# Order of the residual combinations, of one gate pair's operand loads and of a meta token's sums in a one-core encoder kernel

## The chip, the cores and the metric

The kernel runs on one core of a Trainium2 chip. The metric is device microseconds of one execution, lower is better. Before the change three executions took 2128.84, 2129.21 and 2135.24 us (median 2129.21).

## The reference

One encoder layer is applied to two sequences with shared weights: a long one of 1024 tokens and a short one of 512, each with 16 learned meta tokens in front, all in float32. Only what the change touches is quoted; the attention that makes `mix` lies ahead of it.

```python
D_MODEL, D_FF, N_META = 1024, 2816, 16

h = h + mix @ w_out                      # residual add behind the attention
n = rms_norm(h, g_ffn)
gate = n @ w_ff_gate                     # 1024 x 2816
pad = pad_by_one_position(gate)          # zero outside the sequence
gate = pad[:, :-2] * conv_w[0] + pad[:, 1:-1] * conv_w[1] + pad[:, 2:] * conv_w[2] + conv_b
h = h + (gelu(gate) * (n @ w_ff_up)) @ w_ff_down
y = rms_norm(h, g_final)[:, N_META:]     # the meta tokens are dropped at the end
```

Behind the attention only the last meta token still matters: the convolution at the first real token reads its gate.

## The kernel before, in words

Tensors are held transposed, with model columns on the 128 partitions and tokens along the free dimension. Every product is made of three fp32r matmuls: each operand is split into a high part (`split`, L114: a cast on ACT) and a low part (L115: a subtraction on DVE or POOL), and `mm3` (L121 to L123) multiplies high by high, low by high and high by low. The code is written as generators; a scheduler then sets the order of each engine's instructions, and each engine runs its own list strictly in that order. `behind(g, ins)` adds an ordering without a wait: what is issued in its block stands behind `ins` in the list of that instruction's engine.

For the long sequence `mixer_out_long` computes `h + mix @ w_out` in three thirds of each half of the tokens (`PARTS`: 170, 172 and 170 columns of each half, so tiles of 342, 344 and 340 columns). For each of eight row blocks `j` it loads the residual, runs 24 matmuls into a PSUM buffer `s` (there are three), adds the residual on DVE (L728), stores the block for later (L729) and adds up its squares. When a third is done, its generator `combine` takes the mean of squares on PE (L657), the inverse root (L103 to L107), scales the third (L667), and forms the seven operands of one Strassen-Winograd step: `x11, x21, x22` as they are and `t1` to `t4` as differences (L680), each split. `combine` is called `late` and is advanced two steps at a time between the row blocks of the next third, from `j = ML = 2` on. The combination of the last third runs beside the first gate products.

`conv_glu_long` then goes through the 22 blocks of the hidden width in 11 pairs. Each pair needs seven block products for the gate (`winograd`, 12 matmuls each, added up on DVE by L934 and L991) and seven for the up matrix. Gate operands of the first pair have been split and summed earlier and lie in DRAM as `g.wg`; `product` loads each as a high and a low tile of 256 KB (L923), through `HB` = 5 pairs of buffers. The first pair's gate runs in two chunks of columns: 342 columns (of the first two thirds) and 170 columns (of the last third). Each chunk loads all seven operands, 28 loads in all.

The gate of the last meta token is a matrix-vector product made outside of PE's main work: ACT scales the raw gate weights by the token's normalised vector (L977, eight instructions for each block of 128), DVE adds them up over the eight row blocks (L979), and a matmul with a constant column adds over the partitions (L1004). The raw gate weights of the first pair are loaded behind the 18th of the 28 loads (`g.loads[17:18]`).

Of the kernel before, what the change touches and what calls it, by code (L numbers as in the profile page):

```python
# [1 line left out]

# [1 line left out]

# [16 lines left out]
P = 128  # L21
# [618 lines left out]
def mixer_out_long(ctx, g, wp, x, begin):  # L640

    nc = g.nc
    hp = pool(ctx, g, "fh0", 2, "right")
    cm = max(2 * w + 2 * (o == 0) for o, w in PARTS)

    def halves(a, o, w):
        return a.rearrange("... (x t) -> ... x t", x=2)[..., o:o + w]

    def combine(o, w, cw, h, sums):
        ps = g.psum.tile(P, cw, "s")
        for i, sq in enumerate(sums):
            nc.tensor.matmul(ps, lhsT=g.ones_d, rhs=sq, start=i == 0, stop=i == len(sums) - 1)  # L657
        rstd = hp.tile([P, cm], F32, name="rstd", tag="rstd", bufs=1)[:, :cw]
        rsqrt_newton(g, hp, rstd, ps, cw)
        yield  # L660
        if not x:
            xp = begin()
            g.x0 = xp.tile([P, KT], F32, name="x0")
            x.update({nm: [xp.tile([P, HT, H], F32R, name=f"{nm}_{part}") for part in ("hi", "lo")] for nm in XS})
        for k in range(KT):
            hs = h[:, k, :2 * w]
            nc.vector.scalar_tensor_tensor(out=hs, in0=hs, scalar=g.gain[:, V_GFFN + k:V_GFFN + k + 1],  # L667
                                           in1=rstd[:, :2 * w], op0=ALU.mult, op1=ALU.mult)
            if k % 2:
                yield  # L670
        if cw > 2 * w:
            nc.vector.scalar_tensor_tensor(out=g.x0, in0=h[:, :, 2 * w], scalar=rstd[:, 2 * w:2 * w + 1],
                                           in1=g.gain[:, V_GFFN:V_GFFN + KT], op0=ALU.mult, op1=ALU.mult)
        (x11, x12), (x21, x22) = [[h[:, k:k + HT, i * w:(i + 1) * w] for i in range(2)] for k in (0, HT)]

        def kept(nm, src):
            split(g, x[nm][0][:, :, o:o + w], x[nm][1][:, :, o:o + w], src)

        def minus(out, a, b):
            nc.vector.tensor_tensor(out=out, in0=a, in1=b, op=ALU.subtract)  # L680

        kept("x11", x11)
        yield
        kept("x21", x21)
        yield
        minus(x11, x12, x11)
        kept("t1", x11)
        yield
        minus(x11, x22, x11)
        kept("t2", x11)  # L690
        yield
        minus(x12, x22, x12)
        kept("t3", x12)
        yield
        kept("x22", x22)
        minus(x21, x21, x11)
        kept("t4", x21)

    late = None
    with ExitStack() as es:  # L700
        mp = pool(es, g, "fm0", 2, "right")
        for o, w in PARTS:
            cw = 2 * w + 2 * (o == 0)
            xhi, xlo = [[mp.tile([P, cm], F32R, name=nm, tag=f"{nm}{k}", bufs=1 + (k >= KT - 2))[:, :cw] for k in range(KT)]
                        for nm in ("xhi", "xlo")]
            h = hp.tile([P, KT, cm], F32, name="h", tag="h")[:, :, :cw]
            acc = mp.tile([P, cm], F32, name="acc", tag="acc")[:, :cw]
            sums = [acc]

            def loaded(tag, bufs, real, meta):  # L710
                t = mp.tile([P, cm], F32, name=tag, tag=tag, bufs=bufs)[:, :cw]
                nc.sync.dma_start(out=t[:, :2 * w].rearrange("p (x t) -> p x t", x=2), in_=halves(real, o, w))
                if o == 0:

                    nc.sync.dma_start(out=t[:, 2 * w:2 * w + 1], in_=meta)
                    nc.vector.memset(t[:, 2 * w + 1:], 0.0)
                return t

            for k in range(KT - 1, -1, -1):
                rows = g.oT[0][k * P:(k + 1) * P]  # L720
                split(g, xhi[k], xlo[k], loaded("m", MB, rows[:, 1:], rows[:, 0:1]))
            for j in range(KT):
                wj = load_parts(g, wp, g.wo[j]) if j in PRE else load_halves(g, wp, g.w_out[j])
                rows = g.xT[0][j * P:(j + 1) * P]
                res = loaded("res", 2, rows[:, NMETA:], rows[:, NMETA - 1:NMETA])
                ps = g.psum.tile(P, cw, "s")
                dense(g, ps, wj, xhi, xlo, 0, cw, range(KT - 1, -1, -1))
                nc.vector.tensor_tensor(out=h[:, j], in0=ps, in1=res, op=ALU.add)  # L728
                nc.gpsimd.dma_start(out=halves(g.h[j], o, w),  # L729
                                    in_=h[:, j, :2 * w].rearrange("p (x t) -> p x t", x=2))  # L730
                if o == PARTS[-1][0] and j >= KT - 2:

                    sums.append(mp.tile([P, cm], F32, name="sq_p", tag="m", bufs=MB)[:, :cw])
                    nc.scalar.activation(sums[-1], h[:, j], AF.Square)
                else:
                    add_square(g, mp, acc, h, j, 0, cw, nc.gpsimd, 1)
                yield 24 * cw
                if late and j >= ML:
                    for _ in range(2):
                        next(late, None)  # L740
            if late:
                drain(late)
            late = combine(o, w, cw, h, sums)
        next(late)
    return late
# [149 lines left out]
    yield 0  # L895


def winograd(g, wp, up, x, raw, c0, cw, pre=None):

# [14 lines left out]
    def product(a, b, place):  # L916
        if pre is None:
            a = split_half(g, wp, a)
        else:
            i, half = place  # L920
            a = [wp.tile([P, H], F32R, name=nm, tag=nm, bufs=HB) for nm in ("w_hi", "w_lo")]
            for part, tl in enumerate(a):
                g.loads.append(nc.sync.dma_start(out=tl.bitcast(F32),  # L923
                                                 in_=pre[i, part, :, half * H:(half + 1) * H]).ins)
# [31 lines left out]
def conv_glu_long(ctx, g, wp, x, late, es_x, es_h):  # L956
# [6 lines left out]
    up = pool(es, g, "fu0", 2, "left")  # L963
    ap = None
    first = PARTS[-1][0]
    g.loads = []

    def load_gate(f0):


        with behind(g, *g.loads[17:18] if f0 == 0 else g.loads[-1:] if f0 == 2 else []):
            raw = [load_whole(wp, g, g.w_gate[f0 + i]) for i in range(2)]
        sums = []
        for i in range(2):
# [8 lines left out]
    for f0 in range(0, NFF, 2):  # L983
# [2 lines left out]
            raw, first_sums = load_gate(f0)  # L986

        for c0, cw in ((0, first), (first, H - first)) if f0 == 0 else ((0, H),):
            for i, half, ps, rest in winograd(g, wp, up, x, raw if f0 else None, c0, cw, None if f0 else g.wg):
                t0 = 1 + half * H + c0  # L990
                nc.vector.tensor_tensor(out=gate[:, i, t0:t0 + cw], in0=ps, in1=rest, op=ALU.add)  # L991
                for _ in range(3):
# [5 lines left out]
        if not ap:  # L998
            es_h.close()
            ap = pool(es, g, "fa0", 1, "left")  # L1000
        act = ap.tile([P, 2, N], F32, name="act", tag="act", bufs=2)
        for i in range(2):
            ps = g.psum.tile(P, 2, "mm")
            nc.tensor.matmul(ps, lhsT=first_sums[i], rhs=g.ones_d[:, 0:2], start=True, stop=True)  # L1004
# [12 lines left out]
        if f0 + 2 == NFF:  # L1017
            with tc.issue_after(gelu.ins):
                nc.scalar.preload_act_table_set(EXP_LN)
        raw = [load_whole(up, g, g.w_up[f0 + i], "w_f2") for i in range(2)]  # L1020
        for i, half, ps, rest in winograd(g, wp, up, x, raw, 0, H):
            a = act[:, i, half * H:(half + 1) * H]
            nc.vector.tensor_tensor(out=ps, in0=ps, in1=rest, op=ALU.add)
            nc.vector.tensor_tensor(out=a, in0=ps, in1=a, op=ALU.mult)
# [417 lines left out]
```

## Time and profile before

| | us |
|---|---|
| median of three executions | 2129.21 |
| their range | 2128.84 to 2135.24 |
| the profiled execution | 2138.1 |
| its span, first to last instruction | 2136.3 |
| PE busy in the span | 2051.1 (96%) |
| DVE busy | 1724.1 (81%) |
| ACT busy | 1156.8 (54%) |
| POOL busy | 582.7 (27%) |

The profiled execution is 8.9 us longer than the median of the others. PE, TensorE's matmuls, has work nearly all the time, so a microsecond is worth something where PE waits or where its clock is low. The granted clock is given as a share of full speed: 1.00 is 2.4 GHz and 0.50 is 1.2 GHz.

### The profile page before, as it was taken

Reading aid. Unit: us, or ns where it says so; the run is one execution under the profiler, and the core shown is the slowest. Engines: PE = TensorE matmul, PEld = TensorE weight load, DVE = VectorE, ACT = ScalarE, POOL = GpSimd, SP = SyncE. Lnnn points to the kernel's source line nnn. Section 1 sums busy time; section 2 is a strip of 40 time slices with the busy share of each in tenths; the row PEclk is TensorE's granted clock in tenths of the full one; section 3 lists DMA queues with packets and bytes.
Section 4 is the critical chain, followed back from the end, with each engine's and each line's share of the span. In section 5 each row is a group of like instructions: output and inputs, shape, how many; then the busy total and the mean of one; then the engine's idle time right before and its main releaser. Section 6 shows DMA issues by size and latency. Waiting matters only on the chain.

```text
span 2136.3 us, 35264 instructions
## 1 busy us (share of the span) xinstructions
PE 2051.1 (96%) x12302; PEld 1833.1 (86%) x12302; DVE 1724.1 (81%) x3786; ACT 1156.8 (54%) x2253; POOL 582.7 (27%) x534
## 2 busy tenths in 40 slices
PE   6999999999999999999999999979999999999998
PEld 6988888997887999899989999978888777778877
DVE  6878889767879788888988885578878878869886
ACT  6635566544657556666666765345444444435454
POOL 4653233553112000000000000542444444330112
PEclk8999999999999999999999999998999999999999
DMA  7564335456621322223352224986232232247443
GB/s 252 178 198 133 118 110 170 153 182 226 206 84 55 105 75 70 70 85 114 103 188 77 93 88 145 300 256 229 101 109 89 97 115 84 94 166 258 119 126 126
DMA packets 164897, 296.30 MB, mean 139 GB/s; under 512 B 21456, under 2 KB 82672, under 8 KB 164208
## 3 DMA queue, kind: packets, MB, share of 16 engines
q1 hardware_dynamic: 162416, 287.76, 41.6%
q0 software_dynamic: 2304, 6.29, 0.8%
q8 instruction: 97, 1.59, 0.3%
q14 instruction: 80, 0.66, 0.1%
HBM read 211.13 MB, written 82.85 MB: 138 GB/s over the span
## 4 chain that ended last, share of the span: by engine, by line
PE 76%; DVE 12%; DMA 4%; ACT 3%; issue 3%; POOL 1%; SPq 1%; DVEq 0%; ACTq 0%; POOLq 0%
PE ps_mm L121 17%; PE ps_mm L123 17%; PE ps_mm L122 17%; PE ps_t L456 5%; PE ps_s L431 3%; PE ps_s L432 3%; PE ps_s L121 2%; PE ps_s L122 2%; PE ps_s L123 2%; PE ps_o L471 2%; PE ps_o L470 2%; DVE p L433 1%; DVE w_lo L115 1%; DMA m<-oT 1%; DVE acc L979 1%
## 5 line engine op out<-in xcount | busy, mean ns | idle before, releaser
L121 PE MATMUL ps_mm<-xhi,w_hi 128*128 128x258 f32 (+3 forms) x1264 | 383.4, 304 | 12.0 <-ACT xhi L114 3.7
L122 PE MATMUL ps_mm<-xlo,w_hi 128*128 128x258 f32 (+3 forms) x1264 | 379.0, 300 | 0.3 <-POOL xlo L115 0.3
L123 PE MATMUL ps_mm<-xhi,w_lo 128*128 128x258 f32 (+3 forms) x1264 | 377.2, 299 | 0.3 <-DVE w_lo L115 0.3
L433 DVE TENSOR_SCALAR_CACHE_REDUCE p<-ps_s 114x344 f32<-114x344 f32 (+4 forms) x562 | 257.6, 488 | 30.2 <-PE ps_s L432 19.1
L114 ACT CAST pt_hi<-ps_t 128x512 fp32r<-128x512 f32 (+6 forms) x360 | 169.3, 483 | 181.0 <-PE ps_t L456 155.2
L121 PEld LDWEIGHTS ps_mm<-xhi,w_hi 128*128 128x128 f32 x1264 | 240.0, 190 | 17.5 <-ACT xhi L114 5.4
L438 ACT ACTIVATE p<-p,nm 114x1040 f32<-114x1040 f32 (+5 forms) x212 | 214.8, 1013 | 72.8 <-DVE nm L436 71.8
L115 DVE TENSOR_TENSOR w_lo<-w_f,w_hi 128x1024 fp32r<-128x1024 f32 (+1 forms) x182 | 192.8, 1067 | 66.2 <-ACT w_hi L114 65.6
L122 PEld LDWEIGHTS ps_mm<-xlo,w_hi 128*128 128x128 f32 x1264 | 240.3, 190 | 1.9 <-POOL xlo L115 0.7
L123 PEld LDWEIGHTS ps_mm<-xhi,w_lo 128*128 128x128 f32 x1264 | 240.0, 190 | 1.2 <-DVE w_lo L115 0.5
L114 ACT CAST w_hi<-w_f 128x1024 fp32r<-128x1024 f32 (+1 forms) x199 | 167.6, 856 | 84.9 <-PE ps_mm L122 57.5
L115 DVE TENSOR_TENSOR pt_lo<-ps_t,pt_hi 128x512 fp32r<-128x512 f32 (+4 forms) x312 | 171.7, 561 | 43.7 <-ACT pt_hi L114 42.3
L115 POOL TENSOR_TENSOR a_lo<-gate,a_hi 128x256 fp32r<-128x256 f32 x44 | 43.3, 985 | 545.3 <-ACT a_hi L114 525.9
L431 PE MATMUL ps_s<-k,q 128*114 128x348 f32 (+4 forms) x552 | 183.6, 338 | 3.4 <-DVE p L433 3.2
L456 PE MATMUL ps_t<-ident,p 128*128 128x128 f32 (+7 forms) x1188 | 183.0, 270 | 1.0 <-DVE nm L436 0.5
L432 PE MATMUL ps_s<-k,q 128*114 128x348 f32 (+4 forms) x552 | 171.1, 315 | 0.0
L121 PE MATMUL ps_s<-xhi,w_hi 128*128 128x256 f32 (+4 forms) x480 | 148.7, 313 | 20.4 <-ACT xhi L234 8.2
L456 PEld LDWEIGHTS ps_t<-ident,p 128*128 128x128 f32 (+7 forms) x1188 | 140.4, 136 | 29.6 <-issue 6.8
L123 PE MATMUL ps_s<-xhi,w_lo 128*128 128x256 f32 (+4 forms) x480 | 147.4, 307 | 1.4 <-DMA w_lo<-wo 1.4
L122 PE MATMUL ps_s<-xlo,w_hi 128*128 128x256 f32 (+4 forms) x480 | 148.6, 310 | 0.0
L121 PE MATMUL ps_mm<-t_hi,w_hi 128*128 128x512 f32 (+2 forms) x368 | 144.6, 393 | 1.2 <-DVE v L934 1.2
L123 PE MATMUL ps_mm<-t_hi,w_lo 128*128 128x512 f32 (+2 forms) x368 | 144.4, 392 | 0.1
(275 smaller groups left out, 5309.4 us busy)
## 6 DMA issues: line engine op xcount, KB each, us to landing
w_f<-w_gate SPq DMA_DIRECT2D x46, 512.0 KB, 3.5
w_f<-w_up SPq DMA_DIRECT2D x44, 512.0 KB, 3.4
w_f<-w_in SPq DMA_DIRECT2D x36, 512.0 KB, 3.9
a_f<-act SPq DMA_DIRECT2D x62, 256.0 KB, 2.7
w_f<-w_down SPq DMA_DIRECT2D x22, 512.0 KB, 3.3
act<-a_t SPq DMA_DIRECT2D x44, 256.0 KB, 2.1
a<-w_down SPq DMA_DIRECT2D x40, 256.0 KB, 5.4
w_hi<-wo SPq DMA_DIRECT2D x36, 256.0 KB, 5.1
```

The source lines that it names most:

```text
L114: return (nc.scalar.copy(hi, src).ins, (lo_engine or nc.vector).tensor_tensor(out=lo, in0=src, in1=hi.bitcast(F32), op=ALU.subtract).ins)
L115: (lo_engine or nc.vector).tensor_tensor(out=lo, in0=src, in1=hi.bitcast(F32), op=ALU.subtract).ins)
L121: nc.tensor.matmul(ps, lhsT=whi, rhs=xhi, start=start, stop=False)
L122: nc.tensor.matmul(ps, lhsT=whi, rhs=xlo, start=False, stop=False)
L123: return nc.tensor.matmul(ps, lhsT=wlo, rhs=xhi, start=False, stop=stop).ins
L431: nc.tensor.matmul(ps, lhsT=q[0], rhs=k[:, c0:c0 + cw], start=True, stop=False)
L432: nc.tensor.matmul(ps, lhsT=q[1], rhs=k[:, c0:c0 + cw], start=False, stop=True)
L433: nc.vector.tensor_scalar(out=p[:, c0:c0 + cw], in0=ps, scalar1=HD ** -0.5, scalar2=-3.0e38, op0=ALU.mult, op1=ALU.max, accum_out=mx[:, i: ...
L438: g.last_exp = nc.scalar.activation(p, p, AF.Exp, bias=nm, accum_out=l).ins
L456: nc.tensor.transpose(tps[:, c:c + M], p[:, k0:k0 + kw], g.ident[:M, :M])
L470: nc.tensor.matmul(o, lhsT=v[:, i, :], rhs=hi, start=i == 0, stop=False)
L471: nc.tensor.matmul(o, lhsT=v[:, i, :], rhs=lo, start=False, stop=False)
```

## The change

Four edits. The residual add of a row block is remembered as `added`, and the two steps of `combine` that follow it are put behind it. The 14 operand tiles of the first gate pair are kept for the second chunk: five pairs stay in the `w_hi` and `w_lo` buffers, and the other two lie in a third use of the buffers for `h` (`g.spare_h`), which the middle third leaves free. The raw gate weights for the meta token are loaded behind the last of the now 14 loads. The up weights and, for the first pair, the first up product are issued ahead of the matmul L1004.

```diff
+    g.spare_h = lambda: hp.tile([P, KT, cm], F32, name="h", tag="h")
...
-                nc.vector.tensor_tensor(out=h[:, j], in0=ps, in1=res, op=ALU.add)
+                added = nc.vector.tensor_tensor(out=h[:, j], in0=ps, in1=res, op=ALU.add).ins
...
                 if late and j >= ML:
-                    for _ in range(2):
-                        next(late, None)
+                    with behind(g, added):
+                        for _ in range(2):
+                            next(late, None)
...
+        elif place in kept:
+            a = kept[place]
         else:
             i, half = place
-            a = [wp.tile([P, H], F32R, name=nm, tag=nm, bufs=HB) for nm in ("w_hi", "w_lo")]
+            if len(kept) < HB:
+                a = [wp.tile([P, H], F32R, name=nm, tag=nm, bufs=HB) for nm in ("w_hi", "w_lo")]
+            else:
+                a = [more[:, (2 * (len(kept) - HB) + part) * H:][:, :H].bitcast(F32R) for part in range(2)]
+            kept[place] = a
...
-        with behind(g, *g.loads[17:18] if f0 == 0 else g.loads[-1:] if f0 == 2 else []):
+        with behind(g, *g.loads[-1:] if f0 == 0 else g.loads[-1:] if f0 == 2 else []):
             raw = [load_whole(wp, g, g.w_gate[f0 + i]) for i in range(2)]
...
+        raw = [load_whole(up, g, g.w_up[f0 + i], "w_f2") for i in range(2)]
+        products = winograd(g, wp, up, x, raw, 0, H)
+
+        ahead = [next(products)] if f0 == 0 else []
         for i in range(2):
             ps = g.psum.tile(P, 2, "mm")
             nc.tensor.matmul(ps, lhsT=first_sums[i], rhs=g.ones_d[:, 0:2], start=True, stop=True)
...
-        raw = [load_whole(up, g, g.w_up[f0 + i], "w_f2") for i in range(2)]
-        for i, half, ps, rest in winograd(g, wp, up, x, raw, 0, H):
+        for i, half, ps, rest in chain(ahead, products):
```

What the scheduler makes of it differs from the order before only between the middle third of `mixer_out_long` and the first two pairs of `conv_glu_long`. Three places follow. Lines of the changed file stand one to a dozen further down: there L116 is the subtraction L115 of before, L682 is L680, L730 is L728, L989 and L991 are L977 and L979 of the meta token's sums, and L944 and L1003 are the gate's additions L934 and L991.

The first place is DVE at the end of the last third's residual adds (`h_18701`), with the combination of the middle third (`h_18271`) between them. Before:

```order
L728 TENSOR_TENSOR h_18701<-ps_s_19009,res_19007 128x340
L680 TENSOR_TENSOR h_18271<-h_18271 128x4x172
L115 TENSOR_TENSOR t2_lo_18447<-h_18271,t2_hi_18446 128x4x172
L115 TENSOR_TENSOR t4_lo_18453<-h_18271,t4_hi_18452 128x4x172
L728 TENSOR_TENSOR h_18701<-ps_s_19056,res_19054 128x340
L106 SCALAR_TENSOR_TENSOR rstd_19094<-ps_s_19090,eps_133,rstd_19094 128x340
```

and of the change:

```order
L730 TENSOR_TENSOR h_18701<-ps_s_19009,res_19007 128x340
L682 TENSOR_TENSOR h_18271<-h_18271 128x4x172 x2
L116 TENSOR_TENSOR t3_lo_18449<-h_18271,t3_hi_18448 128x4x172
L116 TENSOR_TENSOR t2_lo_18447<-h_18271,t2_hi_18446 128x4x172
L730 TENSOR_TENSOR h_18701<-ps_s_19056,res_19054 128x340
L116 TENSOR_TENSOR x22_lo_18451<-h_18271,x22_hi_18450 128x4x172
L682 TENSOR_TENSOR h_18271<-h_18271 128x4x172
L116 TENSOR_TENSOR t4_lo_18453<-h_18271,t4_hi_18452 128x4x172
L107 SCALAR_TENSOR_TENSOR rstd_19094<-ps_s_19090,eps_133,rstd_19094 128x340
```

Three instructions of the combination went from ahead of the last residual add to behind it, between that add and the last third's inverse root.

The second place is ACT in the combination of the last third (`h_18701`), where it casts the high parts; `prod` is the meta token's scaled weights. Before:

```order
L114 CAST x22_hi_18450<-h_18701 128x4x170
L114 CAST t1_hi_18444<-h_18701 128x4x170
L114 CAST t3_hi_18448<-h_18701 128x4x170
L114 CAST t2_hi_18446<-h_18701 128x4x170
L114 CAST t4_hi_18452<-h_18701 128x4x170
L977 ACTIVATE prod_19401<-w_f_19397,x0_18439 128x128 x8
```

and of the change:

```order
L115 CAST x22_hi_18450<-h_18701 128x4x170
L989 ACTIVATE prod_19370<-w_f_19366,x0_18439 128x128 x8
L115 CAST t1_hi_18444<-h_18701 128x4x170
L115 CAST t3_hi_18448<-h_18701 128x4x170
L989 ACTIVATE prod_19381<-w_f_19368,x0_18439 128x128 x8
L115 CAST t2_hi_18446<-h_18701 128x4x170
L989 ACTIVATE prod_19575<-w_f_19571,x0_18439 128x128 x8
L115 CAST t4_hi_18452<-h_18701 128x4x170
```

The scaled weights, three blocks of them, now stand between the casts of `t1` to `t4`; they stood behind all four.

The third place is DVE in the same stretch, from the first sum into `gate` on. Before:

```order
L991 TENSOR_TENSOR gate_19112<-ps_mm_19136,u_19130 128x342
L115 TENSOR_TENSOR t1_lo_18445<-h_18701,t1_hi_18444 128x4x170
L115 TENSOR_TENSOR t3_lo_18449<-h_18701,t3_hi_18448 128x4x170
L680 TENSOR_TENSOR h_18701<-h_18701 128x4x170
L934 TENSOR_TENSOR u_19130<-ps_mm_19177,u_19130 128x342
L680 TENSOR_TENSOR h_18701<-h_18701 128x4x170
L934 TENSOR_TENSOR v_19191<-ps_mm_19160,u_19130 128x342
L115 TENSOR_TENSOR t2_lo_18447<-h_18701,t2_hi_18446 128x4x170
```

and of the change, from the instruction behind that same sum on:

```order
L991 TENSOR_REDUCE acc_19379<-prod_19370 128x128
L116 TENSOR_TENSOR t1_lo_18445<-h_18701,t1_hi_18444 128x4x170
L116 TENSOR_TENSOR t3_lo_18449<-h_18701,t3_hi_18448 128x4x170
L944 TENSOR_TENSOR u_19131<-ps_mm_19178,u_19131 128x342
L682 TENSOR_TENSOR h_18701<-h_18701 128x4x170
L944 TENSOR_TENSOR v_19192<-ps_mm_19161,u_19131 128x342
L991 TENSOR_REDUCE acc_19390<-prod_19381 128x128
L682 TENSOR_TENSOR h_18701<-h_18701 128x4x170
L944 TENSOR_TENSOR u_19131<-ps_mm_19198,u_19131 128x342
L1003 TENSOR_TENSOR gate_19113<-ps_mm_19198,v_19192 128x342
L1003 TENSOR_TENSOR gate_19113<-ps_mm_19221,v_19192 128x342
L116 TENSOR_TENSOR t2_lo_18447<-h_18701,t2_hi_18446 128x4x170
```

Between the first sum and `t2_lo` there were six instructions; there are now eleven, two of them the meta token's reductions, which stood behind `t4_lo` before. On PE the products of both chunks keep their order, with `t2` and `t3` behind `t1`; L1004 moves from the last gate product to the end of the first up product.

## Rows read from the trace of the kernel before

**Rows 1.** The page: busy time, and the clock in 40 slices of the span.

```profile
PE 2051.1 (96%) x12302; PEld 1833.1 (86%) x12302; DVE 1724.1 (81%) x3786; ACT 1156.8 (54%) x2253; POOL 582.7 (27%) x534
...
PEclk8999999999999999999999999998999999999999
```

**Rows 2.** Busy time by stretch: length, PE, PEld, DVE, ACT, POOL, clock, DMA share, GB/s.

```profile
1462.65:1465.30 2.65, 2.65 (x25) 2.65 (x24) 2.65 (x4) 0.66 (x2) 0.00 (x0) 1.00 0.97 341
1467.00:1477.50 10.50, 10.39 (x49) 10.32 (x49) 8.23 (x13) 6.84 (x21) 0.00 (x0) 0.51 0.85 291
1478.30:1484.30 6.00, 6.00 (x15) 4.74 (x16) 5.90 (x8) 4.63 (x12) 1.28 (x1) 0.51 0.00 1
1484.30:1600.00 115.70, 115.70 (x505) 93.39 (x504) 91.88 (x109) 54.50 (x108) 52.03 (x35) 1.00 0.31 105
```

**Rows 3.** What PE waited for, 1380 to 1500 us: total, times, longest.

```profile
PE ps_s L657 <- DVE h L728: 8.5, 1, 8.5
```

**Rows 4.** PE in order of time: start, us, idle before it and what ended that.

```profile
1446.79 0.73 PE L657 MATMUL ps_s<-sq_p,ones_d 128*128 128x340 f32 x2
1448.53 0.84 PE L657 MATMUL ps_s<-sq_p,ones_d 128*128 128x340 f32 x2 [1.01 <-ACT sq_p L734]
...
1465.18 0.28 PE L123 MATMUL ps_mm<-x_hi,w_lo 128*128 128x170 f32 x1
1466.65 0.32 PE L121 MATMUL ps_mm<-t_hi,w_hi 128*128 128x170 f32 x1 [1.19 <-DVE v L934]
...
1467.18 0.51 PE L123 MATMUL ps_mm<-t_hi,w_lo 128*128 128x170 f32 x1
...
1477.52 0.92 PE L1004 MATMUL ps_mm<-ones_d,acc 128*128 128x2 f32 x4
```

**Rows 5.** DVE in order of time.

```profile
1445.76 1.78 DVE L115 TENSOR_TENSOR t_lo<-h,t_hi 128x688 fp32r<-128x688 f32 x2
1447.46 0.50 DVE L728 TENSOR_TENSOR h<-ps_s,res 128x340 f32<-128x340 f32 x1
1451.03 0.57 DVE L106 SCALAR_TENSOR_TENSOR rstd<-ps_s,eps,rstd 128x340 f32<-128x340 f32 x1 [3.07 <-ACT rstd L105]
...
1462.14 0.50 DVE L991 TENSOR_TENSOR gate<-ps_mm,u 128x342 f32<-128x342 f32 x1
1462.56 1.63 DVE L115 TENSOR_TENSOR t_lo<-h,t_hi 128x680 fp32r<-128x680 f32 x2
1464.11 0.86 DVE L680 TENSOR_TENSOR h<-h 128x680 f32<-128x680 f32 x1
...
1466.51 0.85 DVE L115 TENSOR_TENSOR t_lo<-h,t_hi 128x680 fp32r<-128x680 f32 x1
...
1469.75 1.91 DVE L979 TENSOR_REDUCE acc<-prod 128x128 f32<-128x1024 f32 x1
1471.58 0.33 DVE L991 TENSOR_TENSOR gate<-ps_mm,u 128x170 f32<-128x170 f32 x1
1474.17 1.97 DVE L979 TENSOR_REDUCE acc<-prod 128x128 f32<-128x1024 f32 x1 [2.27 <-ACT prod L977]
```

**Rows 6.** ACT in order of time.

```profile
1456.17 1.43 ACT L114 CAST x_hi<-h 128x680 fp32r<-128x680 f32 x2 [0.83 <-DVE h L667]
1458.82 0.76 ACT L114 CAST t_hi<-h 128x680 fp32r<-128x680 f32 x1 [1.23 <-DVE h L680]
...
1466.87 2.45 ACT L977 ACTIVATE prod<-w_f,x 128x128 f32<-128x128 f32 x8
```

**Rows 7.** DMA issues of SP, 1436 to 1475 us: count, KB each, median us to landing.

```profile
w_hi<-wg SPq DMA_DIRECT2D x14, 256.0 KB, 5.1
w_lo<-wg SPq DMA_DIRECT2D x14, 256.0 KB, 5.3
w_f<-w_gate SPq DMA_DIRECT2D x4, 512.0 KB, 6.2
```

**Rows 8.** SP in order of time: the issue of the first pair's raw gate weights.

```profile
1457.77 0.90 SPq L150 DMA_DIRECT2D w_f<-w_gate  x2
```

More of the change, by code (lines that the diff above doesn't have):

```diff
@@ L1 @@
 from contextlib import ExitStack, nullcontext
+from itertools import chain
 import numpy as np
@@ L895, in presplit, with winograd @@
     yield 0
-def winograd(g, wp, up, x, raw, c0, cw, pre=None):
+def winograd(g, wp, up, x, raw, c0, cw, pre=None, kept=None, more=None):
     nc = g.nc
@@ L965, in conv_glu_long @@
     first = PARTS[-1][0]
-    g.loads = []
+    g.loads, kept = [], {}
+    more = g.spare_h().rearrange("p k c -> p (k c)")
     def load_gate(f0):
-        with behind(g, *g.loads[17:18] if f0 == 0 else g.loads[-1:] if f0 == 2 else []):
+        with behind(g, *g.loads[-1:] if f0 == 0 else g.loads[-1:] if f0 == 2 else []):
             raw = [load_whole(wp, g, g.w_gate[f0 + i]) for i in range(2)]
@@ L988, in conv_glu_long @@
         for c0, cw in ((0, first), (first, H - first)) if f0 == 0 else ((0, H),):
-            for i, half, ps, rest in winograd(g, wp, up, x, raw if f0 else None, c0, cw, None if f0 else g.wg):
+            for i, half, ps, rest in winograd(g, wp, up, x, raw if f0 else None, c0, cw, None if f0 else g.wg, kept, more):
                 t0 = 1 + half * H + c0
```

## The prediction

> **What bounds the kernel now.** I read the page first: PE is busy for 96% of the span and its clock is at nine tenths or more in all slices but the first and the 28th, 1442 to 1495 us [rows 1]. That slice is where the change sits. So the question is what PE waits for there, and why its clock is low. Then I read the stretch table, the waits and the time lines.
>
> Four things stand out. PE waits 8.5 us before the mean square of the middle third [rows 3]. It waits 1.01 us before the last part of the last third's mean square, for the square of the last row block [rows 4]. It waits 1.19 us at the third product of the second chunk, and two matmuls later 0.3 us more: the third matmul starts 0.53 us after the first, and two steps of 0.11 us explain only 0.22 [rows 2, 4]. And from 1467 on the clock is at half, 1.2 GHz, until about 1484. Before the fall PE ran 170-column matmuls and then had these two short waits. Behind 1484 PE is busy without a break at full clock [rows 2], so what is won or lost up to there should reach the end of the kernel.
>
> What the low clock costs is read from rows at either level. At full clock 24 matmuls of 170 columns take 2.65 us, 0.11 each; at half clock 49 take 10.5 us, 0.214 each. That is 5.1 us lost. Of the 512-column ones 15 take 6.0 us, while 505 take 115.7 us at full clock, 0.229 each: 2.6 us lost. Together 7.7 us [rows 2].
>
> **The change, part by part.** Each sum is against the profiled execution, 2138.1 us (span 2136.3), which is 8.9 us above the median of the runs.
>
> *Residual adds ahead of the combination.* Before, the last add L728 starts at 1447.46, behind two splits that DVE began at 1445.76 [rows 5]. PE has only the first parts of the mean square to do then, until 1447.5 [rows 4]. Now three instructions stand behind the add and the chain add, square, last matmul can run about 1.0 us earlier, which is all of the 1.01 us wait: **-1.0**. The three cost little: they fall into the 3.07 us that DVE sat idle before L106 [rows 5]. But they do not fit wholly. The last of them needs a cast on ACT in between, and two splits, a difference and a cast, at 0.8 us each, behind an add that ends near 1446.9 end near 1450.5. So L106 comes about 0.5 us earlier rather than 1.0, and so does all that follows on DVE. The other adds that move forward have no PE wait behind them: counted at nothing. The 8.5 us stay, because DVE's list ahead of them is the same.
>
> *Half of the loads go.* Of 28 loads of 256 KB [rows 7] 14 go, and with them the DMA share of 0.97 to 0.85 in the chunk [rows 2]. What PE gets from that is the 0.3 us behind the third product's second matmul, which waits for a low operand tile: **-0.3**. The 1.19 us ahead of it was put down to DVE's `v`, which frees a PSUM buffer; in the changed program this product takes a buffer that comes free ahead of `v`, so I let this wait go too: **-1.2**, and what is late next is the split of `t1`. The two pairs in the spare buffer can be loaded only behind the middle third's last split, near 1450.5. The first chunk runs from about 1448 at 1.95 us a product (seven from 1449 to 1462.65), so its sixth product needs the first of them near 1457.8; issue to landing takes 5.1 to 5.3 us [rows 7], so they come just in time: 0. On SP the gate load stands behind them.
>
> *The meta token's sums move forward.* The title speaks of PE's matmul L1004, which moves behind an up product. It waits for nothing in this trace at 1477.52 [rows 4], so this gives nothing by itself. But the gate weights are now loaded earlier, and the lists of ACT and DVE take the token's sums earlier with them, into the last third's combination, and there they stand ahead of operands that PE waits for.
>
> When do they run? The gate load is issued behind the spare loads, near 1452.3; with 6.2 us to landing [rows 7] it is there at 1458.5. ACT has cast the last third's `x` near 1457 (1457.6 before [rows 6]), then waits for it, and takes 2.45 us for eight scalings [rows 6], until about 1461. DVE ends the first sum into `gate` at 1462.1 (0.5 us earlier than the next instruction's 1462.56 [rows 5]), so the first reduction need not wait. It occupies DVE for 1.83 us (1469.75 to the next start at 1471.58 [rows 5]).
>
> - `t1`: sum 0.42, reduction 1.83, split 0.85: from 1461.65 to 1464.75. PE is ready for it at 1464.4 (1465.4 before, less 1.0). **+0.4**.
> - `t2`: before, its split starts 4.37 us after the sum (1462.14 to 1466.51 [rows 5]). Now two reductions more (3.66) and three additions more of 0.42 each (1.26) stand between: 9.29 us, so it starts at 1470.95 and ends at 1471.8. PE has finished the third product by then: 1464.8 plus eleven steps of 0.11 is 1466.0. The product of `t3` stands behind it on PE. **+5.8**.
> - `t4`: behind it by two instructions, near 1473.5. PE needs it four products later: 0.
>
> *The clock.* The wait of 5.8 us comes in a stretch of 170-column matmuls, where a shorter one was enough before. I expect the clock to fall in it. Four products, 48 matmuls, then run at half, as 49 did before, and it took until some 15 of 512 columns had passed before the clock was back [rows 2]. So the loss is the same 7.7 us: **0**. Bounds: 7.7 us won if the clock holds; nothing more to lose.
>
> Sum: -1.0 -0.3 -1.2 +0.4 +5.8 = **+3.7 us**, 2141.8 us for an execution like the profiled one. From the median of 2129.21 this gives **2132.9 us**, 0.17% more. About 0.3% (6.4 us) is what a measurement of this kernel can tell from no change.
>
> **The rivals.**
>
> 1. *The ordinary runs of before keep their clock* (slower). Two of three runs lie 6 us under the third, which lies 3 under the profiled one. If the fall at 1467 is marginal and most runs escape it, they save what it cost there: the 2.6 us of the 512-column matmuls, and of the chunk the part up to where L1004 would wait for the second reduction (1474.17 + 1.97 = 1476.14, against 1477.52 [rows 4, 5]), 1.4. Together 4.0 us, while the change's longer wait brings the fall each time: +7.7, **2136.9 us**. It decides where 1.5 us of waiting among 170-column matmuls does not lower the clock. Against it: in the profiled execution it did. The Trainium skill ("TensorE: Matmul & The Clock Gate", section "HAM oscillation — how this bites in real kernels") lays falls to long idle gaps between bursts; by that rule only the change's wait would lower the clock. The trace disagrees for this execution.
>
> 2. *The gate weights land late* (slower). ACT and DVE are held by them. If they landed where the load of before should have, 1457.77 plus 6.2 or 1464.0 [rows 7, 8], the scaling would end at 1466.4 and the reduction start 4.3 us later than above. All behind it moves: +8.0, **2137.2 us**. Against it: 14 loads fewer are ahead of it.
>
> 3. *The clock holds through the new wait*: -7.7, so -4.0 and **2125.2 us**. Falls are rare in the span [rows 1], but this wait is far longer than the one that sufficed.
>
> 4. *The sums do not hold `t2`* (faster): reductions and scalings find gaps, both operands are there in time, and the clock holds: -1.0 -1.5 -7.7 = -10.2, **2119.0 us**. Against it: DVE had no gap from the sum at 1462.14 to 1471.9 [rows 5], and it takes its list strictly in order.
>
> That the change doesn't do what it says is part of my forecast: only the matmul of the sums moves back, their work on two engines moves forward.
>
> **How the numbers follow.** Forecast (within 0.3%) 0.53; rival 1 0.22; rival 2 0.12; rival 3 0.07; rival 4 0.06. So faster 0.06, same 0.53 + 0.07 = 0.60, slower 0.22 + 0.12 = 0.34. The range runs from rival 3 to 2 us over rival 2, for a clock that comes back later: 2125 to 2139 us. It leaves out rival 4 and part of rivals 2 and 3. The forecast's own range is 2131 to 2135.
>
> **What would show it.** The time line of PE should show the last mean-square matmul near 1447.5 with no wait, then in the second chunk a short wait for the split of `t1` and one of 5 to 6 us at a matmul with `t_lo`, with the clock at half from that wait on, for some 15 us. ACT should show the scalings L977 between casts of `t_hi`, with or without a wait for the gate load, and DVE two reductions before the split of `t2`. The forecast is wrong if PE runs through the second chunk, or if the stretch from 1449 to 1500 gets longer by something other than these waits.

## The result, and the profile after

The changed kernel took 2138.14 us (median of 10 executions, 2131.59 to 2140.35), the kernel before beside it 2130.38 us (10 executions, 2128.01 to 2135.24). The ratio is 1.003, with a 95% interval of 1.0019 to 1.004: slower by 0.3%. A second series (12 executions against 35 of before) gave 2135.03 against 2129.67 us, ratio 1.0025 (1.0015 to 1.0035). The forecast was 2132.9 us; the measured time lies where rivals 1 and 2 put it, inside the range. The two profiled executions differ by less: 2140.35 against 2138.1 us. One later execution of the kernel before, 3299.84 us at a mean clock of 0.556, is left out of every figure here.

The page of the changed kernel shows the same picture as [rows 1], with the slice of low clock at 1442 to 1495 us in the same place; the other one has moved from the first slice to the fourth:

```profile
PE 2050.9 (96%) x12302; PEld 1831.3 (86%) x12302; DVE 1724.7 (81%) x3786; ACT 1156.4 (54%) x2253; POOL 582.7 (27%) x534
...
PEclk9998999999999999999999999998999999999999
```

What PE waited for between 1380 and 1500 us in the changed kernel (total, times, longest):

```profile
PE ps_s L659 <- DVE h L730: 8.5, 1, 8.5
...
PE ps_mm L123 <- DVE t_lo L116: 3.8, 2, 3.3
...
PE ps_s L659 <- ACT sq_p L736: 1.6, 1, 1.6
...
PE ps_mm L122 <- ACT t_hi L115: 1.3, 1, 1.3
```

The 8.5 us of [rows 3] are still there. The wait at the last part of the mean square, 1.01 us in [rows 4], did not go; it is 1.55 us. The waits for `v` and for a low weight tile in the second chunk are gone, and waits for `t_hi` and `t_lo` stand in their place. PE of the changed kernel in order of time (the second row is the first product with `t1`, the third and fourth the one with `t2`, the fifth the first up product, the last two the token's matmuls of the first and the second pair):

```profile
1444.77 0.84 PE L659 MATMUL ps_s<-sq_p,ones_d 128*128 128x340 f32 x2 [1.55 <-ACT sq_p L736]
...
1462.16 0.35 PE L123 MATMUL ps_mm<-t_lo,w_hi 128*128 128x170 f32 x1 [0.48 <-DVE t_lo L116]
...
1464.93 0.46 PE L122 MATMUL ps_mm<-t_hi,w_hi 128*128 128x170 f32 x2 [1.30 <-ACT t_hi L115]
...
1469.19 0.51 PE L123 MATMUL ps_mm<-t_lo,w_hi 128*128 128x170 f32 x1 [3.27 <-DVE t_lo L116]
...
1478.46 0.70 PE L122 MATMUL ps_mm<-x_hi,w_hi 128*128 128x512 f32 x1
...
1485.92 0.50 PE L1020 MATMUL ps_mm<-ones_d,acc 128*128 128x2 f32 x4
...
1520.10 0.50 PE L1020 MATMUL ps_mm<-ones_d,acc 128*128 128x2 f32 x4
```

From the last part of the mean square to the first up product it is 33.69 us (1444.77 to 1478.46). Before it was 29.77 (1448.53 in [rows 4] to 1478.30, where a stretch of [rows 2] begins). These two stretches do not hold the same work: in the kernel before the first pair's token matmul lies within, and ten matmuls of the last gate product run only at 1485.27, behind 18 of the up products. Up to the token's matmul of the second pair both kernels have done the same. Before:

```profile
1521.51 0.50 PE L1004 MATMUL ps_mm<-ones_d,acc 128*128 128x2 f32 x4
```

For this same work the changed kernel took 75.33 us (1444.77 to 1520.10) and the kernel before 72.98 (1448.53 to 1521.51), so it lost 2.35 us here. DVE of the changed kernel shows why `t2` is late:

```profile
1458.92 0.51 DVE L1003 TENSOR_TENSOR gate<-ps_mm,u 128x342 f32<-128x342 f32 x1
1459.34 1.99 DVE L991 TENSOR_REDUCE acc<-prod 128x128 f32<-128x1024 f32 x1
1461.26 1.63 DVE L116 TENSOR_TENSOR t_lo<-h,t_hi 128x680 fp32r<-128x680 f32 x2
...
1463.23 0.85 DVE L682 TENSOR_TENSOR h<-h 128x680 f32<-128x680 f32 x1
...
1464.43 1.90 DVE L991 TENSOR_REDUCE acc<-prod 128x128 f32<-128x1024 f32 x1
...
1467.02 0.50 DVE L944 TENSOR_TENSOR u<-ps_mm,u 128x342 f32<-128x342 f32 x1
1467.45 0.92 DVE L1003 TENSOR_TENSOR gate<-ps_mm,v 128x342 f32<-128x342 f32 x2
1468.29 0.85 DVE L116 TENSOR_TENSOR t_lo<-h,t_hi 128x680 fp32r<-128x680 f32 x1
```

Two reductions stand between the first sum into `gate` and the split of `t2`, which now starts 9.37 us behind that sum (1458.92 to 1468.29) and not 4.37 us as in [rows 5]. ACT has the scalings between its casts, and does not wait for the gate weights at the first of them:

```profile
1456.35 2.45 ACT L989 ACTIVATE prod<-w_f,x 128x128 f32<-128x128 f32 x8
1458.71 1.41 ACT L115 CAST t_hi<-h 128x680 fp32r<-128x680 f32 x2
1461.37 2.45 ACT L989 ACTIVATE prod<-w_f,x 128x128 f32<-128x128 f32 x8 [1.25 <-DVE acc L991]
1464.12 0.76 ACT L115 CAST t_hi<-h 128x680 fp32r<-128x680 f32 x1 [0.30 <-DVE h L682]
```

The cast of `t2` at 1464.12, for which PE waits 1.30 us, stands behind the second block of scalings; but what it waits for last, 0.30 us behind them, is DVE's difference L682 at 1463.23, which stands behind the first reduction. So it is DVE's reductions that hold both halves of `t2`; the scalings end sooner. The stretches of the changed kernel (length, busy time of PE, PEld, DVE, ACT, POOL, clock, DMA share, GB/s) show the clock at half from 1465.40 on:

```profile
1444.77:1465.40 20.63, 18.84 (x126) 18.34 (x127) 19.38 (x26) 11.48 (x27) 3.13 (x3) 1.00 0.63 221
1465.40:1478.46 13.06, 9.79 (x46) 9.57 (x46) 10.35 (x19) 7.33 (x16) 3.87 (x3) 0.50 0.08 30
1478.46:1482.40 3.94, 3.94 (x11) 3.07 (x11) 0.34 (x1) 1.24 (x1) 0.00 (x0) 0.50 0.64 206
```

The fall stands between the two waits for `t2`: the first ends at 1464.93, the second, of 3.27 us, begins near 1465.9. So it is not the long wait that came ahead of the fall in this profile, but 0.48 and 1.30 us, hardly more than the 1.19 and 0.3 us in the kernel before.

One more difference lies far behind the change: what PE waited for between 1500 and 2140 us. First the changed kernel,

```profile
PE ps_mm L124 <- DVE w_lo L116: 5.5, 8, 0.9
PE ps_mm L122 <- ACT w_hi L115: 2.3, 1, 2.3
```

then the kernel before:

```profile
PE ps_mm L123 <- DVE w_lo L115: 3.7, 6, 0.7
PE ps_mm L121 <- ACT w_hi L114: 2.3, 1, 2.3
```

So in the later pairs PE waits for a low half of weights, in the changed kernel in two pairs more and 1.8 us longer in all. And at the 2.3 us wait for `w_hi`, which both have, the clock fell in the changed kernel alone. First the changed kernel, then the kernel before:

```profile
1919.00:1926.00 7.00, 6.98 (x24) 5.59 (x25) 4.14 (x7) 3.51 (x6) 0.00 (x0) 0.76 1.05 389
```

```profile
1918.00:1940.00 22.00, 21.95 (x97) 18.16 (x98) 16.37 (x27) 13.33 (x24) 0.00 (x0) 1.00 1.05 388
```

From there to a wait that both have near 2070 us the changed kernel took 1.6 us more (1919.02 to 2071.14, before 1918.05 to 2068.61). The two profiled executions then add up: the changed one reached the last mean square 3.8 us earlier, lost 2.35 up to the second pair's token matmul, 1.8 in the waits for weights and 1.6 at this fall, which is 1.9 of the 2.25 us.

### The profile page after: what moved, and what is told of

Same layout as the page of the kernel before. It is cut to its first block, busy times and chain, and to the rows that moved or that the text cites. A ratio compares the mean times of both kernels' runs of the same rounds, so it can differ in the third digit from the quotient of the medians.

```text
span 2138.5 us, 35240 instructions
## 1 busy us (share of the span) xinstructions
PE 2050.9 (96%) x12302; PEld 1831.3 (86%) x12302; DVE 1724.7 (81%) x3786; ACT 1156.4 (54%) x2253; POOL 582.7 (27%) x534
## 4 chain that ended last, share of the span: by engine, by line
PE 72%; DVE 14%; DMA 5%; issue 4%; ACT 3%; POOL 1%; SPq 0%; DVEq 0%; ACTq 0%; POOLq 0%
PE ps_mm L122 16%; PE ps_mm L124 16%; PE ps_mm L123 16%; PE ps_t L457 5%; PE ps_s L432 3%; PE ps_s L433 3%; DVE w_lo L116 2%; DVE p L434 2%; PE ps_o L472 2%; PE ps_s L122 2%; PE ps_s L123 2%; PE ps_s L124 2%; PE ps_o L471 2%; DMA m<-oT 1%; DVE acc L991 1%
## 5 line engine op out<-in xcount | busy, mean ns | idle before, releaser
L115 ACT CAST pt_hi<-ps_t 128x512 fp32r<-128x512 f32 (+6 forms) x360 | 169.3, 483 | 185.3 <-PE ps_t L457 157.8
L116 DVE TENSOR_TENSOR w_lo<-w_f,w_hi 128x1024 fp32r<-128x1024 f32 (+1 forms) x182 | 193.5, 1070 | 62.3 <-ACT w_hi L115 61.8
L115 ACT CAST w_hi<-w_f 128x1024 fp32r<-128x1024 f32 (+1 forms) x199 | 167.6, 856 | 76.9 <-PE ps_mm L123 52.7
L116 DVE TENSOR_TENSOR pt_lo<-ps_t,pt_hi 128x512 fp32r<-128x512 f32 (+4 forms) x312 | 171.8, 561 | 45.3 <-ACT pt_hi L115 44.0
L116 POOL TENSOR_TENSOR a_lo<-gate,a_hi 128x256 fp32r<-128x256 f32 x44 | 43.3, 986 | 543.4 <-ACT a_hi L115 524.1
L123 PE MATMUL ps_mm<-t_lo,w_hi 128*128 128x512 f32 (+2 forms) x360 | 141.5, 393 | 3.8 <-DVE t_lo L116 3.8
```

The costliest lines, as they stand in the source:

```text
L115: return (nc.scalar.copy(hi, src).ins, (lo_engine or nc.vector).tensor_tensor(out=lo, in0=src, in1=hi.bitcast(F32), op=ALU.subtract).ins)
L116: (lo_engine or nc.vector).tensor_tensor(out=lo, in0=src, in1=hi.bitcast(F32), op=ALU.subtract).ins)
L123: nc.tensor.matmul(ps, lhsT=whi, rhs=xlo, start=False, stop=False)
```

## The experiments

Each run lists its span and its mean granted clock. Of every run I take (1 - clock) x span, by how much the clock was below full over the whole span, and the rest. A wait at half clock counts with half its length in the first of these, though PE does nothing in it; so the split shows where the clock changed and is not the price of the clock. The clock is given to three places (2.1 us), so only the means over a series count; the standard error of a mean of twelve is 0.7 to 1.2 us for the low clock and 0.5 to 0.9 for the rest. For before the executions beside three later series are taken together, for the changed kernel both series. The span is some 1.8 us shorter than the time.

| kernel (executions) | mean us | (1 - clock) x span | rest |
|---|---|---|---|
| before (87) | 2129.3 | 32.0 | 2095.5 |
| before_again (12) | 2127.8 | 29.4 | 2096.6 |
| changed (22) | 2136.0 | 35.2 | 2098.9 |
| kept_only (7) | 2137.2 | 36.6 | 2098.8 |
| adds_only (12) | 2131.4 | 32.5 | 2097.1 |
| up_only (12) | 2129.0 | 30.5 | 2096.7 |
| late_sums (12) | 2128.8 | 31.9 | 2095.0 |
| filled (12) | 2129.7 | 27.8 | 2100.0 |
| late_sums_no_adds (12) | 2127.6 | 27.8 | 2098.0 |
| warm_before (12) | 2129.8 | 28.6 | 2099.5 |
| warm_late (12) | 2125.6 | 23.4 | 2100.5 |

The change costs 6.7 us in these means: 3.2 of low clock and 3.4 of the rest, with standard errors of 0.7 and 0.5.

**Before, once more (before_again).** No edit.

> The kernel before, unchanged, for a second profile. Theory A (the ordinary runs of before keep their clock in the second chunk of the first gate pair): this profiled execution lasts about 2130 us, PE's clock there is 1.00 from the last third's mean square to the up products, and from the first product of the first chunk to the first up product PE takes some 4 to 5 us less than the 29 us of the first profile. Theory B (the fall is there in each run, and what the change costs is lost elsewhere): the clock is at half from the third product of the chunk on as in the first profile, and the 8 us between the profiled execution (2138.1) and the median (2130.4) lie in other stretches.

Median 2127.54 us (ratio 0.9996, 0.9985 to 1.0006); the profiled execution took 2125.24 us, 13 less than the first. PE waits and order of time there:

```profile
PE ps_mm L1004 <- DVE acc L979: 3.1, 1, 3.1
```

```profile
1437.54 0.84 PE L657 MATMUL ps_s<-sq_p,ones_d 128*128 128x340 f32 x2 [0.39 <-ACT sq_p L734]
...
1465.18 0.59 PE L1004 MATMUL ps_mm<-ones_d,acc 128*128 128x2 f32 x2 [3.07 <-DVE acc L979]
1465.63 0.77 PE L121 MATMUL ps_mm<-x_hi,w_hi 128*128 128x512 f32 x1
...
1508.33 0.50 PE L1004 MATMUL ps_mm<-ones_d,acc 128*128 128x2 f32 x4
```

PE runs through the second chunk with no wait of over 0.3 us, and with the clock high it comes to the token's matmul early and waits 3.07 us for the second reduction. The clock falls in that wait, and its low time costs PE only this much:

```profile
1437.54:1460.20 22.66, 22.14 (x149) 21.13 (x149) 20.06 (x29) 9.64 (x20) 4.62 (x3) 1.00 1.02 370
...
1465.63:1470.10 4.47, 4.47 (x12) 3.50 (x13) 4.41 (x9) 2.09 (x5) 1.29 (x1) 0.50 0.04 15
```

The 512-column matmuls of these 4.47 us start 0.43 us apart, and 0.23 us at full clock, so about 2 us are lost, where the first profile lost 7.7. The stretch up to the first up product takes 28.09 us against 29.77, the one up to the second pair's token matmul 70.79 (1437.54 to 1508.33) against 72.98. So theory A holds for the chunk, but not to its full size: the fall only moves behind a wait that the low clock had hidden. The other 11 us between the two profiles lie ahead of the last mean square (1448.53 against 1437.54). The mean clocks, 0.982 and 0.987, put about as much to low clock over the span (38.5 against 27.6 us).

**The sums behind `t4` (late_sums).**

```diff
-        kept("t4", x21)
+        g.t4 = split(g, x["t4"][0][:, :, o:o + w], x["t4"][1][:, :, o:o + w], x21)
...
+            with behind(g, *(g.t4 if f0 == 0 else [])):
+                for k in range(KT):
+                    nc.scalar.activation(prod[:, k], raw[i][:, k * P:(k + 1) * P], AF.Copy, scale=g.x0[:, k:k + 1])
+                nc.vector.tensor_reduce(out=acc, in_=prod.rearrange("p k c -> p c k"), axis=AX.X, op=ALU.add)
```

> The changed kernel with the meta token's scalings and reductions of the first pair put behind the split of t4 on ACT and DVE. Theory A (the loss is the wait for t2's operands, 1.30 and 3.27 us, that these sums cause, and the fall of the clock that the wait brings each time): both waits go, the clock mostly holds, and the median is 2125 to 2130 us, 8 to 13 us under the changed kernel's 2138.1. Theory B (the loss lies in the order of the residual adds or in the kept operands, and the clock falls in any case): the median stays at 2135 or more. Theory C (the waits go, but the splits of the weights in the later pairs set the pace there and give back most of what is won): PE's waits for low halves of weights behind 1500 us grow by some 3 to 5 us over the changed kernel's 5.5, and the median is 2132 to 2136 us.

2128.23 us, ratio to before 1.0001 (0.9988 to 1.0014): the whole loss is gone. The kept operands and the earlier gate load are still there, so it is the place of the sums that costs. Of the waits for `t2` one of 1.7 us is left:

```profile
PE ps_mm L123 <- DVE t_lo L116: 1.7, 1, 1.7
```

The waits for low halves of weights behind 1500 us are 3.6 us, not more than before, so theory C fails and theory A holds. In the profiled execution the clock fell behind these 1.7 us all the same (0.57 from 1470 to 1475 us).

**The kept operands and the earlier gate load alone (kept_only).** The changed kernel with `behind(g, added)` and `ahead` taken out again.

> The kernel before with the kept operands and the earlier gate load alone: the residual adds and the first up product are ordered as before. The meta token's reductions stand ahead of t1 and t2 here too. Theory A: PE waits 4 us or more for t2's operands, and the median is 2136 to 2140 us, as for the whole change. Theory B (the order of the residual adds or the first up product is the cause): the median is within 2 us of before, 2128 to 2132 us.

2135.97 us, ratio 1.0038 (1.0022 to 1.0054): these two edits carry the loss. Here the first reduction stands ahead even of two of the three splits of `x`, and the waits have moved accordingly; together they are 4.4 us, where 4 or more for `t2` alone were expected:

```profile
PE ps_mm L122 <- ACT t_hi L115: 1.9, 1, 1.9
PE ps_mm L123 <- DVE x_lo L116: 1.4, 1, 1.4
...
PE ps_mm L123 <- DVE t_lo L116: 1.1, 1, 1.1
```

**The residual adds alone (adds_only).**

```diff
+                added = nc.vector.tensor_tensor(out=h[:, j], in0=ps, in1=res, op=ALU.add).ins
...
+                    with behind(g, added):
+                        for _ in range(2):
+                            next(late, None)
```

> The kernel before with the combinations behind the residual adds alone. The reductions stand behind t4 as before. Theory A: within 2 us of before, 2128 to 2132 us, without a wait of over 1.5 us for a split of t1 or t2; the last part of the mean square comes at most 1 us earlier. Theory B (the order of the residual adds is the cause): 2135 us or more, with DVE's list ahead of the last third's scaling longer than before, so that the first product of t1 or t2 in the second chunk waits 3 us or more.

2132.13 us, ratio 1.0013 (0.9998 to 1.0029): 0.1 us over theory A's range, far under theory B's, and not told from no change. The longest wait for a split of `t1` or `t2` is 0.7 us, as theory A has it. The wait at the last part of the mean square is 0.5 us, about what before_again shows without this edit (0.4).

**The first up product alone (up_only).** The part of the change with `products`, `ahead` and `chain` in the kernel before.

> The kernel before with the first up product ahead of the token's matmul and nothing else. In the second profile of before that matmul waited 3.1 us for the second reduction, with the clock at full by then; in the first one it waited for nothing, because the clock was low and PE late. If that wait is what the edit saves, the median is 2125 to 2127 us, 2 to 3 us under before, with no wait of that matmul. If the wait goes to the up product (its weights' low halves stand behind the reductions on DVE): within 1 us of before.

2128.87 us, ratio 0.9996 (0.9984 to 1.0007): nothing, as the second case has it. PE no longer waits for the reduction, but for the up product's own operands, which ACT and DVE make behind the sums:

```profile
1470.53 0.79 PE L122 MATMUL ps_mm<-x_hi,w_hi 128*128 128x512 f32 x1 [1.39 <-ACT w_hi L115]
...
1472.86 0.80 PE L124 MATMUL ps_mm<-x_hi,w_lo 128*128 128x512 f32 x1 [1.11 <-DVE w_lo L116]
```

**The wait filled (filled).** In `winograd`, in the second chunk of the first pair, behind the `t1` product:

```diff
+    if pre is not None and c0:
+        fill = g.psum.tile(P, H, "mm")
+        for i in range(24):
+            with behind(g, g.last_mm):
+                g.last_mm = nc.tensor.matmul(fill, lhsT=block(kept[0, 0], i % HT)[0], rhs=x["x21"][0][:, i % HT],
+                                             start=i == 0, stop=i == 23).ins
     s2 = s_(ALU.subtract, s1, a11)
-    p6 = product(s2, x["t2"], (1, 1))
+    with behind(g, *([g.last_mm] if pre is not None and c0 else [])):
+        p6 = product(s2, x["t2"], (1, 1))
```

`g.last_mm` is the matmul that was issued last.

> The changed kernel with 24 matmuls of 512 columns, whose result nothing reads, on PE between the t1 and the t2 product of the second chunk: about 5.1 us of work in a place where the changed kernel waits 1.30 + 3.27 us for t2's operands. What PE waits for is as late as before, but PE is not idle. Theory A (about half of the loss is the wait itself and half the clock that falls because of it): the clock stays at 1.00 from 1462 us to the up products, nearly no wait is left for t2, and the median is 2132 to 2135 us, 3 to 6 us under the changed kernel's 2138.1. Rival (the clock falls there whatever PE does, or the fall costs nothing because PE would wait for the reductions or the weights anyway): 2137 to 2140 us.

2129.44 us, ratio to before 1.0002 (0.9991 to 1.0014). PE in order of time, and the stretch with the added matmuls:

```profile
1458.66 5.82 PE L956 MATMUL ps_mm<-x_hi,w_hi 128*128 128x512 f32 x24
...
1469.79 0.43 PE L122 MATMUL ps_mm<-x_hi,w_hi 128*128 128x512 f32 x1
```

```profile
1458.66:1469.79 11.13, 11.13 (x74) 9.87 (x73) 11.10 (x18) 7.12 (x18) 1.28 (x1) 1.00 0.15 49
```

The operands are as late as in the changed kernel, yet the clock holds and the stretch from the last mean square (1440.00) to the first up product is 29.79 us, not 33.69. The table says the same: the rest stays as high as in the changed kernel (2100.0), and 7.4 us of low clock go. That is more than the 3.2 that the change had added; before has low clock in this place too, in both of its profiles, and the time fell lower than theory A had it.

**The changed kernel, once more (after_again).** No edit.

> The changed kernel, unchanged, for a second profile and more times. Theory A: median 2136 to 2139 us, a wait of 4 us or more for t2's operands in the second chunk and the clock at half from there to the up products, 15 us or more. Rival (the first profile was an unlucky one): median near 2133 us, and the clock comes back within 7 us.

2135.03 us. The waits are those of the first profile (0.34, 1.30 and 3.47 us for `t1` and `t2`), and the stretch is 33.66 us (1439.83 to 1473.49). The clock came back some 2 us behind its end, after about 14 us. The median is 1 us under theory A's range.

**The sums late, the residual adds as before (late_sums_no_adds).** late_sums without `behind(g, added)`.

> The kernel before with kept operands and the first up product ahead, the token's sums behind the split of t4, and the residual adds ordered as before. With late_sums (2128.2 us) it prices the order of the residual adds alone. If that order costs what the run of it alone suggested (+3 us, interval 0 to 6): 2123 to 2126 us. If it costs nothing: 2127 to 2130 us.

2127.61 us, ratio to before 0.9989 (0.9978 to 1.0): the order of the residual adds costs nothing that can be told from late_sums. Its profile shows PE's shortest way so far, 24.31 us from the last mean square (1442.27) to the first up product, at full clock with one wait of 0.73 us. Up to the second pair's token matmul (L1019 in this file) it is 65.50 us (1442.27 to 1507.77), 5.3 us less than in before_again for the same work, yet the median is only about 2 us under before (0 to 4.7 by the interval). Part of the difference is to be seen in the waits behind 1500 us:

```profile
PE ps_mm L124 <- DVE w_lo L116: 5.9, 10, 0.9
```

```profile
1507.77 0.50 PE L1019 MATMUL ps_mm<-ones_d,acc 128*128 128x2 f32 x4
```

Ten waits for a low half of weights and not seven (3.9 us in before_again): PE runs ahead of DVE's splits and is held there.

**The 8.5 us filled (warm_before, warm_late).** Ahead of the middle third's mean square, in the kernel before and in late_sums_no_adds:

```diff
+        if o == PARTS[1][0]:
+            fill = g.psum.tile(P, cw, "t")
+            for i in range(14):
+                with behind(g, g.last_mm):
+                    g.last_mm = nc.tensor.matmul(fill, lhsT=g.ones_d, rhs=h[:, i % 4], start=i == 0, stop=i == 13).ins
```

> The kernel before with 14 fp32 matmuls of 344 columns on PE, whose result nothing reads, ahead of the mean square of the middle third, where PE waits 8.5 us in every profile so far: at 0.57 us each (the two parts of a mean square start 0.57 us apart) they fill 8.0 us of it. In all profiles the clock falls in this wait and is at half for about 10 us behind it. Theory (a wait costs by the clock that falls with it, besides by its length): the wait stays as long, the clock holds, and some 4 to 5 us are won: 2124 to 2126 us. Rival (the time at half costs nothing here, because DVE's combinations set the pace up to the first gate product): within 1 us of before, with longer waits for DVE or ACT behind it.

2130.22 us, ratio 1.0001 (0.9989 to 1.0013): the rival. The clock holds there, and 3.4 us of low clock go from the table, but the rest grows by 4.0. Half of the low clock around this wait had cost PE nothing, because it lay in the wait itself. In before_again, first the wait, then what follows it (0.30 of 8.50 us and 0.43 of 5.90 us, 2.5 us each):

```profile
1405.60:1414.10 8.50, 0.01 (x1) 0.03 (x1) 8.26 (x12) 3.15 (x5) 0.39 (x1) 0.70 0.74 231
1414.10:1420.00 5.90, 5.90 (x21) 5.43 (x22) 3.46 (x6) 2.78 (x6) 3.96 (x5) 0.57 0.59 178
```

What was left to win is about gone again: PE is now early at the last third's mean square, where it waits 2.0 us, and at the token's matmul (L1010 in this file):

```profile
PE ps_mm L1010 <- DVE acc L985: 3.1, 1, 3.1
PE ps_s L663 <- ACT sq_p L740: 2.0, 1, 2.0
```

> The same 14 matmuls in the kernel with kept operands, the first up product ahead and the token's sums behind the split of t4 (2127.6 us without them). Theory: 2122 to 2125 us, faster than both kernels. Rival: 2127 to 2129 us.

2125.86 us, ratio 0.9978 (0.9966 to 0.9990): 0.2% faster than before and faster than the changed kernel, though less than expected. Of the low clock 4.4 us go against late_sums_no_adds, and the rest grows by 2.5. The intervals of the two overlap (0.9978 to 1.0 without the 14 matmuls), so that these matmuls won time is not shown.

## Why the forecast was near and still too low

- *What moved, and where it waits: right.* The sums stand ahead of `t2` on both engines, PE waits for the high part and then the low part of `t2`, and the clock falls there. In the first profile it fell between the two waits (1465.40) and not in the long one, where I expected it; in after_again it fell in the long one (0.67 from 1461.2 to 1461.8). late_sums and kept_only show that this is the cause: with the sums behind `t4` the loss is gone, and the two edits that bring them forward carry it alone.
- *Term by term, for the profiled execution.* `t1`: +0.4 forecast, 0.48 measured. `t2`: +5.8 forecast, 1.30 + 3.27 = 4.57 measured; DVE's part came as summed (9.29 us from the sum to the split, 9.37 measured), and from the end of the `t1` product (near 1463.5) to the end of that split (1469.14) it is 5.7 us; but PE had five matmuls that it could run meanwhile (1464.93 to 1465.50), where the forecast let the whole product of `t3` stand behind that of `t2`. The -0.3 and -1.2 came: both waits are gone. These four make +3.55. At half clock PE was busy for 13.7 us (9.79 + 3.94) and not 16.4 (10.39 + 6.00 in [rows 2]), which wins about 1.3. That leaves +2.25, against 2.35 measured for the same work.
- *The -1.0 of the residual adds: wrong.* I counted the three instructions that went behind the last add. Directly ahead of it two splits still stand, as in [rows 5], and the wait grew from 1.01 to 1.55 us. One profile each has 0.5 and 0.4 with and without this edit, so no effect of this edit shows here.
- *The clock, "0": the step that failed.* Between the two profiled executions it was near: the half-clock stretch is 17.0 us (1465.40 to 1482.40) against some 17 in [rows 2], and 2.7 us less of it is work. But I carried the difference over to the median as if each run of before lost 7.7 us there. before_again lost about 2, and took 2.2 us less for the same work (70.79 against 72.98). That is rival 1, with another end than its own: PE does not keep its clock, it waits 3.07 us at L1004, and the clock falls later and for less. Over the executions the change adds 3.2 us of low clock, where the forecast has 0. The times lie nearer the rival: +7.8 and +5.4 us against the forecast's +3.7 and the rival's +7.7. The range holds them because it was drawn out to the rivals; the forecast's own 2131 to 2135 does not hold 2138.14.
- *"What is won or lost up to there should reach the end": wrong.* In the first profile of before PE waits once in each pair from the sixth to the tenth for a low half of weights, the first time at 1697 us (with one later, six waits, 3.7 us). late_sums_no_adds shows time won ahead of this that is in part given back in these waits, and up_only and warm_before show it given back sooner, in the first pair or just ahead of it; the changed kernel shows 1.8 us more of these waits.
- *Rival 2 (gate weights late): refuted.* They were issued near 1449.6 and the first scaling at 1456.35 waited for nothing. Rivals 3 and 4 did not come.
- *The Trainium skill on the clock* ("TensorE: Matmul & The Clock Gate", section "HAM oscillation — how this bites in real kernels") lays falls to long idle gaps. The runs agree for the 8.5 us wait, in which the clock falls in before_again. They disagree in that 1.7 us in the profile of late_sums was enough, as 1.19 us and 0.3 us behind it were in the first profile. Nor does the length of the gap settle it here: the clock stayed at 1.00 behind a wait of 2.86 us among 512-column matmuls (before_again, 1905.58), and fell behind one of 2.35 us in the same place of the changed kernel (1919.02).

What stays open: how the 6.7 us of the means split between the wait for `t2`, the fall of the clock and the later waits for weights. No run here takes the one away without moving the others.

## What to carry to other kernels

An earlier load can cost time through the work that it sets free: the scheduler put the token's sums, needed last, ahead of operands that PE needed next, on two engines that run their lists in order. When an edit brings data forward, look at what becomes ready with it, and pin it behind what is urgent. And a profile that is slower than the median of the runs is a poor base: ask which of its losses the ordinary runs share before an equal loss is set against it. PE at 96% busy is no proof that PE sets the pace: in warm_before 3.4 us less of low clock left the time as it was, with PE waiting elsewhere instead.

## What the hardware showed beyond the forecast

The same program's clock falls differ from run to run: two profiles of before, 2138.1 and 2125.24 us, stand 13 us apart, and (1 - clock) x span has a mean of 32.0 us in before. Matmuls whose result nothing reads are a way to keep the clock in a wait: 24 of 512 columns in place of 4.6 us of waiting (1.30 + 3.27) took 7.4 us off the changed kernel's (1 - clock) x span, 14 in fp32 in an 8.5 us wait 3.4 and 4.4. In filled they gave 6 us against the changed kernel; in warm_before they gave none, and what they gave in warm_late (1.7 us against late_sums_no_adds) is not clear of the noise. A wait of some 2 us brought the fall in some profiles only: at the wait for `w_hi` between 1905 and 1920 us the clock fell in the changed kernel (2.35 us), kept_only (1.9) and late_sums_no_adds (2.2), and it stayed at 1.00 in both profiles of before (2.27 and 2.86), in late_sums (2.2) and in after_again (2.1).
